# The opening three projections of a hybrid decoder trunk computed pair by pair, and whole-block products pinned in order

## The chip, the cores and the metric

The kernel runs on one core of one Trainium2 chip. The metric is the device time of one execution, in microseconds (us). The engines named here are TensorE (PE for its matmuls, PEld for its weight loads), VectorE (DVE), ScalarE (ACT), GpSimd (POOL) and the engine that issues most DMAs (SP).

## The reference

Four layers, each a token mixer (gated convolution, chunked spatial gating, retention, gated convolution) and a SwiGLU FFN, with RMSNorm ahead of each and at the end. Sequence 512, width 1024, float32. Cut to what matters:

```python
def short_conv_mixer(h, w_in, conv_w, w_out):          # layers 0 and 3
    b_gate, c_gate, z = jnp.split(h @ w_in, 3, axis=-1)
    conv = depthwise_causal_conv3(c_gate * z, conv_w)
    return (b_gate * conv) @ w_out

def swiglu_ffn(h, w_gate, w_up, w_down):
    return (jax.nn.silu(h @ w_gate) * (h @ w_up)) @ w_down

def reference(x, ...):
    for i in range(4):
        x = x + mixer[i % 3](rmsnorm(x, norm_mix_g[i]))
        x = x + swiglu_ffn(rmsnorm(x, norm_ffn_g[i]), ...)
    return rmsnorm(x, final_norm_g)
```

## The kernel before

**Layout.** Activations are held transposed, features on the 128 partitions and the 512 tokens along the free dimension. The residual x is four tiles `x[k]` of 128x1024, each a pair of blocks (two blocks of 128 features, 512 tokens each). So a product over all of x has eight blocks, numbered 0 to 7.

**Split operands.** Every operand is held as a rounded high part and the low remainder. `split` (line 172) makes both: ACT casts the high part, DVE subtracts it from the source for the low part. A product of two operands is three matmuls: high x high, high x low, low x high. `product` (line 182) writes them for a list of blocks into one PSUM bank: for all blocks but the last high x high and high x low, then the weights' low part for all of these, then the three of the last block.

**Two forms of the projections.** A "chunk" of weights covers two blocks of output columns. `columns4` (line 265) computes it by whole blocks: two products of eight blocks, 512 columns, 24 matmuls each. `columns7` (line 220) is a Strassen-like form with seven parts of 256 columns, 12 matmuls each; it needs sums of the blocks of x (`xt`, with parts `th`, `tl`, made in `operand_sums`, line 413) and sums of the weights (`sums`, made in `prepare7`, lines 136 to 139), both made on DVE and split like the rest. The first chunk of each projection in every convolution and FFN is by whole blocks (m = 0; for the FFN the gate `pg` and the up projection `pu`, for the convolution `pc`, `pz` and `pb`), as is one chunk of `pz` at m = 2 of layer 0; the others are seven-part products. The last part of a seven-part product is put off (`self.late`) until `finish` is called.

**Between stages.** `leave` (line 436) computes the eight output blocks of a stage (`out`), adds each to x on DVE (line 457) and at once makes the next stage's operand of it: ACT scales it into `xg` (line 403), `split` makes `xh` and `xl` of it, and for each pair `operand_sums` follows. Squares of x are summed beside it for the norm (lines 318 to 327); the norm's scale itself is applied behind the projections. These temporaries (`xg`, `xt`, the squares) share three buffers (`tmp`).

**Order.** The kernel is written as one stream; a planner of the framework (`schedule_with_timeline_sim=True`) decides at build time, from its own estimate of when each instruction is ready and from priorities, in which order each engine's queue gets its instructions, and which buffer each tile takes. Each engine then works through its queue in that order. `issue_after(ins)` pins what a block of code issues on the engine of `ins` behind `ins`, in issue order alone. `keep_in_program_order` pins the norm's matmuls. Weights are prepared up to four chunks ahead (`weights`, line 147), within four raw buffers, four buffers each for the high and low parts (`wp`), and four more for the parts of the seven-part form that need no sums (`w7`). PSUM has six banks for products (`mm`).

**The opening.** `run` loads x in order and, between its pairs, the weights of the first chunk of `pc` in four pieces (`first_weights`), so that `pc` can begin on the first pair. The chunks of `pz` and `pb` follow by the usual way. The sums of x and the squares follow on ACT behind the last operand (`self.begun`).

Of the kernel before, what the change touches and what calls it, by code (L numbers as in the profile page):

```python
# [11 lines left out]
F32 = mybir.dt.float32  # L12
F32R = mybir.dt.float32r
# [4 lines left out]
P = 128  # L18
# [24 lines left out]
class Kernel:  # L43
    def __init__(self, ctx, tc, a):
        self.tc, self.nc, self.a = tc, tc.nc, a
        pool = lambda name, bufs, **kw: ctx.enter_context(tc.tile_pool(name=name, bufs=bufs, **kw))
        self.const = pool("const", 1)
        self.xp = pool("xp", 1)
        self.opp = pool("opp", 16)
        self.raw = pool("raw", 4)  # L50
        self.wp = pool("wp", 4)
        self.tmp = pool("tmp", 3)
        self.mcp = pool("mcp", 4)
        self.small = pool("small", 1)
        self.mm = pool("mm", 6, space=PSUM)
        self.aux = pool("aux", 1, space=PSUM)
        self.rps = pool("rps", 1, space=PSUM)
        self.chunks, self.ready, self.next = [], {}, 0
        self.late = self.w7 = None
        self.sevens = 2  # L60
        self.held = []

# [53 lines left out]
    def prepare7(self, i):  # L116


        nc = self.nc
        src, _, plain = self.chunks[i]  # L120
        out = [[] for _ in range(8)]
        for half in range(2):
            if plain:
                raw = self.raw.tile([P, 4, NB // 4, P], F32, tag="raw", name=f"raw{i}{half}")
                h, l = (self.wp.tile([P, 4, NB // 4, P], F32R, tag=part, name=f"w{part}{i}{half}") for part in "hl")
                if i:
                    nc.sync.dma_start(raw, src[half])
                    self.split(raw, h, l)
                else:
                    self.first.append((raw, src[half], h, l))  # L130
                for j in range(4):
                    out[j] += [(h[:, j, k], l[:, j, k]) for k in range(NB // 4)]
                continue
            raw = self.raw.tile([P, 4, NB // 4, P], F32, tag="raw", name=f"raw{i}{half}")
            sums = self.sums.tile([P, 4, NB // 4, P], F32, tag="sums", name=f"sums{i}{half}")
            nc.sync.dma_start(raw, src[half])
            nc.vector.tensor_add(sums[:, :2], raw[:, 3:].broadcast_to([P, 2, NB // 4, P]), raw[:, :3:2])  # L137
            nc.vector.tensor_add(sums[:, 2], sums[:, 1], raw[:, 0])
            nc.vector.tensor_add(sums[:, 3], sums[:, 2], raw[:, 1])  # L139
            for x, n, first, pool in ((raw, 3, 0, self.w7), (sums, 4, 3, self.wp)):  # L140
                h, l = (pool.tile([P, n, NB // 4, P], F32R, tag=part, name=f"w{part}{i}{half}{n}") for part in "hl")
                self.split(x[:, :n], h, l)
                for j in range(n):
                    out[first + j] += [(h[:, j, k], l[:, j, k]) for k in range(NB // 4)]
        return out
# [17 lines left out]
        self.next += 1  # L163
        return self.ready.pop(i)

    def first_weights(self, i, j):

        raw, src, h, l = (t[:, j : j + 2] for t in self.first[i])
        self.nc.sync.dma_start(raw, src)
        self.split(raw, h, l)  # L170

    def split(self, src, h, l):

# [8 lines left out]
    def product(self, ps, terms, first=True, last=True, more=False):  # L182


        nc = self.nc
        seq = []
        for lh, ll, rh, rl in terms[:-1]:
            seq += [(lh, rh), (lh, rl)]
        seq += [(ll, rh) for lh, ll, rh, rl in terms[:-1]]
        lh, ll, rh, rl = terms[-1]  # L190
        seq += [(lh, rh), (lh, rl), (ll, rh)]
        for i, (x, y) in enumerate(seq):
            nc.tensor.matmul(  # L193
                ps, x, y, start=first and i == 0, stop=last and i == len(seq) - 1, skip_group_check=more
            )

    def columns(self, name, acts):

# [21 lines left out]
    def columns7(self, name, then, hold=False):  # L220


        nc = self.nc
        w = self.weights()
        c1, c5, c2 = (self.acc(name + n)[:, :H] for n in "152")
        m1, u2, m5 = (self.mcp.tile([P, H], F32, tag="mc", name=name + "m") for i in range(3))
        xs, xt = self.xs, self.xt

        def part(ps, slot, op, at, first):
            at = slice(at * H, (at + 1) * H)  # L230
            self.product(
                ps,
                [(*w[slot][k], o[0][:, at], o[1][:, at]) for k, o in enumerate(op)],
                first,
                more=not first,
            )

        def add(out, ps, m):
            with self.tc.high_priority(SOON):
                nc.vector.tensor_add(out, ps, m)  # L240

        part(c1, 0, xs, 1, True)
        nc.scalar.copy(m1, c1)
        part(c5, 4, xt, 0, True)
        nc.scalar.copy(m5, c5)
        self.finish(hold)
        y = self.temp(name + "y")
        part(c1, 5, xt, 2, False)
        nc.scalar.copy(u2, c1)
        part(c2, 1, xs, 3, True)  # L250
        add(y[:, H : 2 * H], c2, m1)
        part(c5, 6, xs, 2, False)
        add(y[:, :H], c5, u2)
        part(c1, 3, xt, 1, False)
        with self.tc.high_priority(SOON):
            nc.vector.scalar_tensor_tensor(y[:, 2 * H : 3 * H], c1, -1.0, m5, ALU.mult, ALU.subtract)

        def end():
            part(c1, 2, xt, 3, False)
            nc.scalar.mul(y[:, 3 * H :], c1, -1.0)  # L260
            self.held.append(partial(then, y))

        self.late = end

    def columns4(self, name, then, hold=False, kept=True):


        nc = self.nc
        w = self.weights()
        self.finish(hold)  # L270
        out = []
        for even, odd in ((0, 1), (3, 2)):
            ps = self.acc(name)
            terms = []
            for k, (h, l) in enumerate(self.xs):
                terms += [(*w[even][k], h[:, :T], l[:, :T]), (*w[odd][k], h[:, T:], l[:, T:])]
            self.product(ps, terms)
            out.append(ps)
        y = self.hid.tile([P, 2 * T], F32, tag="hid", name=name + "y") if kept else self.temp(name + "y")
        for b in range(2):  # L280
            nc.scalar.copy(y[:, b * T : (b + 1) * T], out[b])
        self.held.append(partial(then, y))

    def finish(self, hold=False):

# [277 lines left out]
        else:  # L563
            self.leave(hid, g, seven)

    def conv(self, j, g, seven, start=False):
        nc = self.nc
        self.r = None
        cw = self.conv_w
# [28 lines left out]
            self.split(y, h, l)  # L598
            acts.extend([(h[:, :T], l[:, :T]), (h[:, T:], l[:, T:])])

        for m in range(NB // 2):
            form = self.columns7 if m else self.columns4
            form("pc", first)
            if m == 3:
# [1 line left out]
            if start and m == 2:  # L606
                form = partial(self.columns4, kept=False)
            form("pz", partial(second, m), m == 0)
            if start and m == 0:
                with self.tc.issue_after(self.begun.ins):  # L610
                    for k in range(NB // 2):
                        self.operand_sums(k, 0)
                    for k in range(NB // 2):
                        self.squares(self.x[k])
            form = self.columns7 if m else self.columns4
            form("pb", third, start and m == 0)
        before = acts[2:]
        begun = [self.begin("out", before) for _ in range(BEGUN)]
        self.finish()
# [217 lines left out]
    def run(self):  # L837
        nc, a = self.nc, self.a
        for i in range(DEPTH):
            j, kind = divmod(i, 3)  # L840
            if kind == 0:
                for m in range(NB // 2):
                    for part in (1, 2, 0):
                        self.plan7(a["conv_w_in"][j, part * NB // 2 + m], m == 0 or (i, m, part) == (0, 2, 2))
                        if m == 3 and part == 1:
# [47 lines left out]
        for _ in range(WARM):  # L893
            nc.tensor.matmul(warm, self.mean_d, self.mean_d, start=True, stop=True)
        nc.scalar.copy(self.const.tile([P, 1], F32, name="first"), self.mean_d[:, :1])
        self.first = []
        self.ready[0] = self.prepare(0)
        for k in range(half):
            if k:
                nc.sync.dma_start(  # L900
                    self.x[k].rearrange("p (b t) -> p b t", b=2),
                    a["x"][2 * k * P : 2 * (k + 1) * P, :].rearrange("(b p) t -> p b t", b=2),
                )
                self.operand(2 * k, 0)
                self.begun = self.operand(2 * k + 1, 0)
                self.first_weights(*((1, 0), (0, 2), (1, 2))[k - 1])
            else:
                for b in range(2):
                    nc.sync.dma_start(self.x[0][:, b * T : (b + 1) * T], a["x"][b * P : (b + 1) * P, :])
                    self.operand(b, 0)  # L910
                    if b == 0:
                        self.first_weights(0, 0)
        nc.sync.dma_start(self.conv_w, a["conv_w"])
        with self.dense():
            self.conv(0, 1, True, True)
            self.ffn(0, 2, False)
        with self.mixed():
            self.sgu(0, 3, True)
# [93 lines left out]
```

## Time and profile before

| what | value |
|---|---|
| median of three runs | 2432.98 us (2431.72 to 2434.72) |
| the profiled execution | 2432.58 us, of which the span is 2430.7 us |
| mean granted TensorE clock | 0.997 of 2.4 GHz |
| PE busy | 2413.3 us, 99% of the span |
| weight loads (PEld) busy | 2166.7 us, 89% |
| DVE busy | 1807.2 us, 74% |
| ACT busy | 1131.8 us, 47% |

The span runs from the first to the last instruction of the one core; all times below are counted from its start. Matmuls overlap, and the busy time of one is longer than its distance to the next, so how fast PE really goes is read from the starts in the timeline and from the counts in a stretch. The granted clock of a stretch is a share of 2.4 GHz; it has two levels, 1.00 and 0.50 (1.2 GHz). An idle time stands in square brackets with what ended it.

### The profile page before, as it was taken

To read this page: it belongs to the slowest core of one execution; us is meant where nothing else is said; L and a number is where in the kernel's file an instruction comes from. 1 tells how busy PE (TensorE), PEld (TensorE's weight loads), DVE (VectorE), ACT (ScalarE), POOL (GpSimd) and SP (SyncE) were. 2 spreads that over 40 slices of the span, in tenths; PEclk is the share of its full clock that TensorE was granted. 3 is DMA by queue.
4 is the path that set the end of the run, shared out by engine and by line. 5 is a ranking of instruction groups with operands and counts; after the bars stand their busy time and mean duration, and the time that the engine had idled before them with its cause. 6 is when DMAs were issued, how large, how long until landed. Compare 5 with 4: busy or idle time off the path is not lost.

```text
span 2430.7 us, 36335 instructions
## 1 busy us (share of the span) xinstructions
PE 2413.3 (99%) x14668; PEld 2166.7 (89%) x14668; DVE 1807.2 (74%) x2617; ACT 1131.8 (47%) x1628; POOL 53.0 (2%) x58
## 2 busy tenths in 40 slices
PE   9999999999999999999999999999999999999998
PEld 8988999988888899999888888899999898899998
DVE  8978978863757888777565464888777897978875
ACT  6545445443324544445433333545445654545444
POOL 0000000000101000000000000000000000000000
PEclk9999999999999999999999999999999999999999
DMA  4232333233333233233222232223233223233231
GB/s 157 93 125 61 118 109 103 88 117 119 96 105 95 74 111 120 87 105 122 91 74 87 74 111 76 95 96 114 91 109 105 87 79 135 73 113 104 91 119 53
DMA packets 79129, 242.02 MB, mean 100 GB/s; under 512 B 8816, under 2 KB 12912, under 8 KB 78960
## 3 DMA queue, kind: packets, MB, share of 16 engines
q1 hardware_dynamic: 77728, 238.61, 30.6%
q8 instruction: 115, 1.88, 0.3%
q10 hardware_dynamic: 1232, 1.09, 0.1%
q14 instruction: 54, 0.44, 0.1%
HBM read 237.56 MB, written 2.10 MB: 99 GB/s over the span
## 4 chain that ended last, share of the span: by engine, by line
PE 96%; DVE 3%; ACT 1%; issue 0%; DMA 0%; SPq 0%; DVEq 0%; ACTq 0%
PE out L193 28%; PE pu L193 22%; PE pg L193 22%; PE pv L193 7%; PE pb L193 3%; PE pc L193 3%; PE pz L193 3%; PE q L193 2%; PE k L193 2%; PE po L193 1%; DVE wl L174 1%; PE ps L697 1%; PE ps L193 1%; DVE x L457 0%; PE rps L384 0%
## 5 line engine op out<-in xcount | busy, mean ns | idle before, releaser
L174 ACT CAST wh<-raw 128x768 fp32r<-128x768 f32 (+3 forms) x502 | 429.2, 861 | 623.8 <-PE out L193 197.3
L174 DVE TENSOR_TENSOR wl<-raw,wh 128x768 fp32r<-128x768 f32 (+3 forms) x502 | 488.5, 985 | 150.4 <-ACT wh L174 147.2
L193 PE MATMUL out<-hidl,wh 128*128 128x512 f32 (+1 forms) x736 | 278.3, 381 | 0.0
L174 ACT CAST wh<-sums 128x1024 fp32r<-128x1024 f32 x194 | 201.1, 1050 | 163.9 <-DVE sums L139 77.9
L193 PE MATMUL out<-hidh,wh 128*128 128x512 f32 (+1 forms) x736 | 274.7, 381 | 0.0
L174 DVE TENSOR_TENSOR wl<-sums,wh 128x1024 fp32r<-128x1024 f32 x194 | 233.7, 1219 | 16.6 <-ACT wh L174 9.2
L193 PE MATMUL out<-hidh,wl 128*128 128x512 f32 (+1 forms) x736 | 204.9, 380 | 0.0
L193 PE MATMUL pg<-xh,wh 128*128 128x256 f32 (+1 forms) x672 | 202.4, 318 | 1.3 <-ACT xh L174 1.3
L193 PE MATMUL pu<-xh,wh 128*128 128x256 f32 (+1 forms) x672 | 200.9, 316 | 0.0
L193 PE MATMUL pg<-xl,wh 128*128 128x256 f32 (+1 forms) x672 | 200.7, 315 | 0.0
L193 PE MATMUL pu<-xl,wh 128*128 128x256 f32 (+1 forms) x672 | 200.1, 314 | 0.0
L457 DVE TENSOR_TENSOR x<-out,x 128x512 f32<-128x512 f32 x192 | 130.5, 685 | 81.2 <-PE out L193 80.9
L193 PE MATMUL pg<-th,wh 128*128 128x256 f32 x640 | 168.6, 284 | 2.5 <-ACT wh L174 2.5
L193 PE MATMUL pg<-tl,wh 128*128 128x256 f32 x640 | 168.7, 284 | 0.0
L193 PE MATMUL pu<-tl,wh 128*128 128x256 f32 x640 | 168.0, 283 | 0.0
L193 PE MATMUL pu<-th,wh 128*128 128x256 f32 x640 | 167.9, 283 | 0.0
L193 PEld LDWEIGHTS out<-hidl,wh 128*128 128x128 f32 x736 | 138.6, 188 | 24.8
L193 PEld LDWEIGHTS out<-hidh,wh 128*128 128x128 f32 x736 | 137.9, 188 | 24.5
L193 PEld LDWEIGHTS out<-hidh,wl 128*128 128x128 f32 x736 | 136.0, 188 | 26.2
L193 PE MATMUL pu<-xh,wl 128*128 128x256 f32 (+1 forms) x672 | 153.2, 313 | 0.0
L193 PE MATMUL pg<-xh,wl 128*128 128x256 f32 (+1 forms) x672 | 149.5, 313 | 0.0
L137 DVE TENSOR_TENSOR sums<-raw 128x512 f32<-128x512 f32 x194 | 130.2, 685 | 15.5 <-DMA raw<-in_ffn_w_up 13.4
(270 smaller groups left out, 5533.6 us busy)
## 6 DMA issues: line engine op xcount, KB each, us to landing
raw<-in_ffn_w_gate SPq DMA_DIRECT2D x88, 512.0 KB, 3.5
raw<-in_ffn_w_up SPq DMA_DIRECT2D x88, 512.0 KB, 3.6
raw<-in_ffn_w_down SPq DMA_DIRECT2D x96, 384.0 KB, 3.3
raw<-in_conv_w_in SPq DMA_DIRECT2D x46, 512.0 KB, 3.9
raw<-in_sgu_w_v SPq DMA_DIRECT2D x16, 512.0 KB, 3.5
raw<-in_sgu_w_u SPq DMA_DIRECT2D x16, 512.0 KB, 3.5
raw<-in_sgu_w_out SPq DMA_DIRECT2D x16, 512.0 KB, 3.5
raw<-in_ret_w_qk SPq DMA_DIRECT2D x16, 512.0 KB, 3.5
```

The lines of the kernel that those rows point to most:

```text
L137: nc.vector.tensor_add(sums[:, :2], raw[:, 3:].broadcast_to([P, 2, NB // 4, P]), raw[:, :3:2])
L174: return self.nc.scalar.copy(h, src), self.nc.vector.tensor_sub(l, src, h.bitcast(F32))
L193: nc.tensor.matmul(ps, x, y, start=first and i == 0, stop=last and i == len(seq) - 1, skip_group_check=more)
L457: nc.vector.tensor_add(x[:, s], ps, x[:, s])
L697: nc.tensor.matmul(ps[:, c * P : (c + 1) * P], v[m // 4][c][:, col], ws[grp // 4][:, at], start=True, stop=True)
```

## The change

The first chunks of the three projections of layer 0 are no longer three `columns4` after one another. A new function, `begin_all`, goes through the four pairs of x; for each it loads the two blocks of x and the three projections' weights of that pair (256 KB each, in runs of 512 bytes), splits them, and adds the pair's contribution to six accumulators, two for each projection: 36 matmuls a pair. For two blocks the matmuls now come as three of the one and three of the other. `blocks_out` copies the accumulators out and holds the follow-up work, as `columns4` did. The sums of x and the squares are issued behind the last operand, as before, from `conv`. The three chunks leave the list of planned weights.

Apart from that, each product of a `columns4` is now pinned on PE behind the product that went before it in the same stage (`self.whole`), across projections, and all parts of the next `columns7` are pinned behind the last of them. This holds wherever `columns4` stands: at the start of the four FFNs and of the convolution of layer 3, and at the one chunk of `pz` in layer 0.

```diff
+    def begin_all(self, srcs):
+        nc = self.nc
+        out = [[self.acc("first") for _ in range(2)] for _ in srcs]
+        parts = []
+        for k in range(NB // 2):
+            half, at = divmod(k, NB // 4)
+            if at == 0:
+                parts = [
+                    [self.wp.tile([P, 4, NB // 4, P], F32R, tag=part, name=f"w{part}f{k}") for part in "hl"]
+                    for _ in srcs
+                ]
...
+            for n, src in enumerate(srcs):
+                raw = self.raw.tile([P, 4, P], F32, tag="raw", name=f"rawf{k}{n}")
+                h, l = (t[:, :, at] for t in parts[n])
+                if n == 0:
+                    for b in range(2):
+                        m = 2 * k + b
+                        nc.sync.dma_start(self.x[k][:, b * T : (b + 1) * T], self.a["x"][m * P : (m + 1) * P, :])
+                        self.begun = self.operand(m, 0)
+                        if b == 0:
+                            nc.sync.dma_start(raw, src[half][:, :, at])
+                            self.split(raw, h, l)
+                else:
+                    nc.sync.dma_start(raw, src[half][:, :, at])
+                    self.split(raw, h, l)
+                xh, xl = self.xs[k]
+                for ps, blocks in zip(out[n], ((0, 1), (3, 2))):
+                    terms = [
+                        (h[:, j], l[:, j], xh[:, b * T : (b + 1) * T], xl[:, b * T : (b + 1) * T])
+                        for b, j in enumerate(blocks)
+                    ]
+                    self.product(ps, terms, k == 0, k == NB // 2 - 1)
+        return out
...
@@ columns7
+        after, self.whole = self.whole, None
+
         def part(ps, slot, op, at, first):
             at = slice(at * H, (at + 1) * H)
-            self.product(
...
+            with self.tc.issue_after(after.ins) if after else nullcontext():
+                self.product(
...
@@ columns4
-            self.product(ps, terms)
+            with self.tc.issue_after(self.whole.ins) if self.whole else nullcontext():
+                self.whole = self.product(ps, terms)
...
@@ conv
-        for m in range(NB // 2):
+        if start:
+            for name, out, then in zip(("pc", "pz", "pb"), start, (first, partial(second, 0), third)):
+                self.blocks_out(name, out, then)
+            with self.tc.issue_after(self.begun.ins):
+                for k in range(NB // 2):
+                    self.operand_sums(k, 0)
+                for k in range(NB // 2):
+                    self.squares(self.x[k])
+        for m in range(1 if start else 0, NB // 2):
...
@@ run
-                for m in range(NB // 2):
+                for m in range(0 if i else 1, NB // 2):
...
-        self.first = []
-        self.ready[0] = self.prepare(0)
-        for k in range(half):
...
-                self.first_weights(*((1, 0), (0, 2), (1, 2))[k - 1])
...
+        first = self.begin_all([a["conv_w_in"][0, part * NB // 2] for part in (1, 2, 0)])
         nc.sync.dma_start(self.conv_w, a["conv_w"])
         with self.dense():
-            self.conv(0, 1, True, True)
+            self.conv(0, 1, True, first)
```

## Rows read from the trace of the kernel before

**Rows 1.** The page's table of busy time, share of the span, instructions.

```profile
PE 2413.3 (99%) x14668; PEld 2166.7 (89%) x14668; DVE 1807.2 (74%) x2617; ACT 1131.8 (47%) x1628; POOL 53.0 (2%) x58
```

**Rows 2.** The page's chain that ended last, by engine.

```profile
PE 96%; DVE 3%; ACT 1%; issue 0%; DMA 0%; SPq 0%; DVEq 0%; ACTq 0%
```

**Rows 3.** PE's timeline, opening: start, duration (us), engine, line, operation, operands, idle before.

```profile
5.61 0.62 PE L193 MATMUL pc<-xh,wh 128*128 128x512 f32 x1
...
10.71 0.50 PE L193 MATMUL pc<-xh,wh 128*128 128x512 f32 x1 [1.00 <-ACT xh L406]
...
42.27 0.28 PE L193 MATMUL pc<-xh,wh 128*128 128x256 f32 x1
42.39 0.28 PE L193 MATMUL pc<-xl,wh 128*128 128x256 f32 x1
```

**Rows 4.** PE's timeline, first FFN's start, up to the norm's matmuls.

```profile
182.35 0.39 PE L193 MATMUL pg<-xh,wh 128*128 128x512 f32 x1
182.58 0.39 PE L193 MATMUL pg<-xl,wh 128*128 128x512 f32 x1
...
211.22 0.95 PE L366 MATMUL scale<-mean_d,sum 128*128 128x1 f32 x8
```

**Rows 5.** Stretches: length, PE, PEld, DVE, ACT, POOL busy (instructions), clock, DMA share, GB/s.

```profile
90.00:100.00 10.00, 10.00 (x75) 9.51 (x74) 7.46 (x11) 4.32 (x7) 0.00 (x0) 1.00 0.05 15
120.00:130.00 10.00, 8.59 (x51) 7.47 (x50) 10.00 (x16) 4.84 (x7) 0.00 (x0) 1.00 0.39 120
182.40:190.30 7.90, 7.89 (x37) 6.25 (x35) 7.17 (x12) 3.97 (x5) 0.00 (x0) 1.00 0.48 139
190.30:193.60 3.30, 1.41 (x7) 1.10 (x8) 2.54 (x5) 3.30 (x6) 0.00 (x0) 1.00 0.52 151
193.60:197.10 3.50, 3.50 (x10) 2.80 (x9) 3.31 (x5) 3.50 (x6) 0.00 (x0) 0.51 0.00 0
2075.00:2081.20 6.20, 4.30 (x13) 3.30 (x13) 5.25 (x8) 6.20 (x9) 0.00 (x0) 0.73 0.27 87
```

**Rows 6.** Timelines of ACT and DVE, first FFN's start: x's scaling, casts, low parts.

```profile
188.27 1.34 ACT L403 ACTIVATE xg<-x,gain 128x512 f32<-128x512 f32 x2 [3.93 <-DVE sum L322]
...
190.45 1.99 ACT L174 CAST wh<-sums 128x1024 fp32r<-128x1024 f32 x2
...
192.99 1.29 DVE L174 TENSOR_TENSOR xl<-xg,xh 128x512 fp32r<-128x512 f32 x2 [0.73 <-ACT xh L174]
...
197.35 0.69 DVE L174 TENSOR_TENSOR xl<-xg,xh 128x512 fp32r<-128x512 f32 x1
...
198.29 0.68 DVE L174 TENSOR_TENSOR xl<-xg,xh 128x512 fp32r<-128x512 f32 x1
```

**Rows 7.** Timelines: a 1024-wide split; other starts: first matmul, last low parts, one cast.

```profile
16.98 1.23 DVE L174 TENSOR_TENSOR wl<-raw,wh 128x1024 fp32r<-128x1024 f32 x1 [0.19 <-ACT wh L174]
...
809.07 0.39 PE L193 MATMUL pg<-xh,wh 128*128 128x512 f32 x1
...
815.55 0.69 DVE L174 TENSOR_TENSOR xl<-xg,xh 128x512 fp32r<-128x512 f32 x1
...
1552.10 0.39 PE L193 MATMUL pg<-xh,wh 128*128 128x512 f32 x1
...
1560.06 1.29 DVE L174 TENSOR_TENSOR xl<-xg,xh 128x512 fp32r<-128x512 f32 x2
...
1897.16 0.39 PE L193 MATMUL pc<-xh,wh 128*128 128x512 f32 x1
...
1900.98 1.06 ACT L174 CAST wh<-raw 128x1024 fp32r<-128x1024 f32 x1 [0.94 <-PE pc L193]
...
1910.68 1.29 DVE L174 TENSOR_TENSOR xl<-xg,xh 128x512 fp32r<-128x512 f32 x2
...
2067.20 0.39 PE L193 MATMUL pg<-xh,wh 128*128 128x512 f32 x1
...
2082.20 0.68 DVE L174 TENSOR_TENSOR xl<-xg,xh 128x512 fp32r<-128x512 f32 x1
```

More of the change, by code (lines that the diff above doesn't have):

```diff
@@ L59, in __init__ @@
         self.late = self.w7 = None
+        self.whole = None
         self.sevens = 2
@@ L125, in prepare7 @@
                 h, l = (self.wp.tile([P, 4, NB // 4, P], F32R, tag=part, name=f"w{part}{i}{half}") for part in "hl")
[L126 to L130, printed above, removed]
+                nc.sync.dma_start(raw, src[half])
+                self.split(raw, h, l)
                 for j in range(4):
@@ L164, in weights, with blocks_out @@
         return self.ready.pop(i)
[L166 to L170, printed above, removed]
+    def begin_all(self, srcs):
[9 more added lines that the diff above has]
+                ]
+            xs = []
+            for n, src in enumerate(srcs):
[11 more added lines that the diff above has]
+                    nc.sync.dma_start(raw, src[half][:, :, at])
+                    self.split(raw, h, l)
+                xh, xl = self.xs[k]
[6 more added lines that the diff above has]
+        return out
+    def blocks_out(self, name, out, then, kept=True):
+        y = self.hid.tile([P, 2 * T], F32, tag="hid", name=name + "y") if kept else self.temp(name + "y")
+        for b in range(2):
+            self.nc.scalar.copy(y[:, b * T : (b + 1) * T], out[b])
+        self.held.append(partial(then, y))
     def split(self, src, h, l):
@@ L192, in product @@
         for i, (x, y) in enumerate(seq):
-            nc.tensor.matmul(
+            mm = nc.tensor.matmul(
                 ps, x, y, start=first and i == 0, stop=last and i == len(seq) - 1, skip_group_check=more
             )
+        return mm
     def columns(self, name, acts):
@@ L227, in columns7 @@
         xs, xt = self.xs, self.xt
+        after, self.whole = self.whole, None
         def part(ps, slot, op, at, first):
             at = slice(at * H, (at + 1) * H)
-            self.product(
[L232 to L236, printed above, removed]
+            with self.tc.issue_after(after.ins) if after else nullcontext():
+                self.product(
+                    ps,
+                    [(*w[slot][k], o[0][:, at], o[1][:, at]) for k, o in enumerate(op)],
+                    first,
+                    more=not first,
+                )
         def add(out, ps, m):
@@ L276, in columns4 @@
                 terms += [(*w[even][k], h[:, :T], l[:, :T]), (*w[odd][k], h[:, T:], l[:, T:])]
-            self.product(ps, terms)
+            with self.tc.issue_after(self.whole.ins) if self.whole else nullcontext():
+                self.whole = self.product(ps, terms)
             out.append(ps)
[L279 to L282, printed above, removed]
+        self.blocks_out(name, out, then, kept)
     def finish(self, hold=False):
@@ L564, in ffn, with conv @@
             self.leave(hid, g, seven)
-    def conv(self, j, g, seven, start=False):
+    def conv(self, j, g, seven, start=()):
         nc = self.nc
@@ L608, in conv @@
             form("pz", partial(second, m), m == 0)
[L609 to L614, printed above, removed]
             form = self.columns7 if m else self.columns4
-            form("pb", third, start and m == 0)
+            form("pb", third)
         before = acts[2:]
@@ L895, in run @@
         nc.scalar.copy(self.const.tile([P, 1], F32, name="first"), self.mean_d[:, :1])
-        self.first = []
-        self.ready[0] = self.prepare(0)
-        for k in range(half):
[L899 to L905, printed above, removed]
-                self.first_weights(*((1, 0), (0, 2), (1, 2))[k - 1])
[L907 to L912, printed above, removed]
+        first = self.begin_all([a["conv_w_in"][0, part * NB // 2] for part in (1, 2, 0)])
         nc.sync.dma_start(self.conv_w, a["conv_w"])
         with self.dense():
-            self.conv(0, 1, True, True)
+            self.conv(0, 1, True, first)
             self.ffn(0, 2, False)
```

## The prediction

> **What bounds the kernel now.** I read the page's busy table first: TensorE (PE) is busy 99% of the span [rows 1]; the chain that ended last is 96% PE [rows 2]. So the kernel's time is PE's work plus the places where PE stands. A busy PE can hide lost time, so I then read PE's own timeline for the distance between starts: 512-column matmuls follow each other every 0.227 us (182.35 to 182.58), 256-column ones every 0.120 us (42.27 to 42.39) [rows 3, 4]. Against that pace the lost time lies in few places. (1) The opening: 144 whole-block matmuls (three projections of 48) run from 5.61 to 42.27 us, 36.66 us, where 144 x 0.2267 = 32.64 would do, so 4.0 us are lost; the largest hole is 1.00 us at 10.71, waiting for x [rows 3]. (2) From 120 to 130 us PE is busy 8.59 of 10 [rows 5]. (3) The start of the first FFN (stage "F0"): from 182.35 to the norm's matmuls at 211.22 are 28.87 us for 96 whole-block and 24 part matmuls, 96 x 0.2267 + 24 x 0.120 = 24.64, so 4.2 us are lost [rows 4]. In 190.30 to 193.60 PE is busy only 1.41 us, and behind it, 193.60 to 197.10, the granted clock is 0.51, that is 1.2 instead of 2.4 GHz [rows 5]. (4) The last FFN ("F3") repeats this near 2075 to 2081 (4.30 us busy of 6.20, mean clock 0.73) [rows 5], and I price it alike. The starts of the FFNs of layers 1 and 2 ("F1", "F2") and of layer 3's convolution ("C3") lose nothing now.
>
> **Why those starts go well now.** Each whole-block product needs the eight blocks of x in turn: 14 matmuls (high x high, high x low) for blocks 0 to 6, then 7 of the weights' low part, then three for block 7. The blocks of the new x leave DVE and ACT late. In F0 PE begins at 182.35 [rows 4], but the low parts of blocks 4 and 5 start on DVE at 192.99, of block 6 at 197.35 and of block 7 at 198.29 [rows 6]. PE bridges these 16 us because the planner lets it take from all four products (two gate, two up) whatever block is there, then parts of the next seven-part product; 37 matmuls run in 182.40 to 190.30 [rows 5]. The lateness is DVE's and ACT's: DVE is busy 7.17 of those 7.90 us [rows 5], and ACT's scaling of blocks 4 and 5 at 188.27 had waited 3.93 us for a temporary that a DVE sum holds [rows 6].
>
> **The change, part by part.**
>
> *Opening.* The loads go pair by pair, and each pair of x feeds 36 matmuls (8.2 us) instead of 12, so after the first pair PE no longer waits for x. The first matmul needs the same two 256 KB loads and stays at 5.61. I leave 0.5 us of waits in the first pair and take 3.5 of the 4.0 us at the end of this block. Added: weights split in twelve 512-wide pieces instead of four such and four 1024-wide ones; with 0.68 us per 512-wide subtraction [rows 6] and 1.23 per 1024-wide one [rows 7] DVE does 12 x 0.68 - 4 x 0.68 - 4 x 1.23 = 0.5 us more, beside PE. The sums of x for the seven-part form start only when x's last pair is in, and wait on ACT behind its scaling; queued behind them on ACT and DVE are the next chunk's weights. SP's later weight loads stand behind x and the twelve small loads; PE has 8 us of work per pair to cover these. Further on DVE decides: it is busy all 10 us of 120 to 130, where PE stands 1.4 us, and idle 2.5 us in 90 to 100 [rows 5]. So the gain lies between 0 and 4.0 us; I take 2.8, since DVE's idle time ahead of its dense stretch can move forward with PE.
>
> *Products in order.* No instruction is added; the pins fix PE's issue order. Behind a matmul that waits for block 4 now stand all later whole products and the seven-part product, and PE has nothing else. The first product covers 14 + 7 = 21 matmuls, 4.8 us, before it needs block 7, and 13 matmuls, 2.9 us, before block 6's low part. If the blocks come when they come now, the first product ends 0.23 us (its low part) + 7 x 0.227 + 3 x 0.227 = 2.5 us after block 6's low part, and the others follow without stop, since their blocks are all there.
> - F0: block 6 is written at 197.35 + 0.69 = 198.04 [rows 6], the first product ends at 200.6 instead of 182.35 + 24 x 0.2267 = 187.8: 12.8 us late. The 4.2 us lost now go, so +8.6.
> - F1: begins 809.07; block 7's low part is written at 815.55 + 0.69 = 816.24, needed at 809.07 + 22 x 0.2267 = 814.06: +2.2 [rows 7].
> - F2: begins 1552.10; blocks 6 and 7 start on DVE at 1560.06 as a pair of 1.29, so block 6 is done by 1560.7, product at 1563.2 instead of 1557.5: +5.7 [rows 7].
> - C3: begins 1897.16; the pair starts at 1910.68, block 6 done by 1911.4, product at 1913.9 instead of 1902.6: +11.3 [rows 7].
> - F3: begins 2067.20; block 6 done at 2082.88 [rows 7]: 12.8 late, less 4.2: +8.6.
>
> These sum to 36.4 us. Less what the new order moves out of the operands' way: in F0 ACT casts two weight sums, 1.99 us, at 190.45 just ahead of blocks 4 and 5 [rows 6]; they can start because the spread-out order frees weight buffers early, and will now come later, -2.0 each in F0 and F3. In C3 ACT's cast at 1900.98 (1.06 us) has waited for PE's pc [rows 7] and its subtraction of 1.23 follows; -2.3. Together 30.1 us. From below these waits cost nothing (blocks within 2.9 and 4.8 us; then F0's and F3's 4.2 us each are gained), from above 36.4; I stay near the top, since the rows of DVE and ACT that make the blocks late don't depend on PE's order, but for the casts named.
>
> *Clock.* The drop in F0 came right behind 3.30 us in which PE was busy 1.41 [rows 5]. Four starts (F0, F2, C3, F3) would now stand 5 to 12 us with still less work. One such stretch of 3.5 us at half clock costs 1.7 us of matmul time; I take one for each start, 4 x 1.7 = 6.8 (the drops of today are inside the 4.2 us already subtracted). Bounds: 0, if the slow stretch falls where PE waits anyway, and two stretches each, 13.6. The Trainium skill (TensorE: Matmul & The Clock Gate, section "What's actually happening") says that the slow clock is the default and that only sustained activity releases it, so an order that makes PE stand pays again when it resumes. By that rule the four drops are certain, as in F0's row; without it the sum would be 6.8 us lower.
>
> **Sum.** -2.8 + 30.1 + 6.8 = +34.1 us on the profiled execution's 2432.6, which is 0.4 below the median of the three runs: 2466.7 us.
>
> **Rivals.**
> - *The blocks arrive in time* (faster). All engines are planned anew; if with PE's demand in order the planner puts x's blocks ahead of the weights' preparation, the holes of F0 and F3 go and none comes: -2.8 - 8.4 = -11.2, 2421.4 us. It decides at 2.9 us for block 6 and 4.8 us for block 7 after the first matmul of the stage. For it: F1 misses it by only 2.2 us. Against it: F0 misses by 12.8 us, with DVE nearly full and ACT held by a buffer, which no pin on PE frees.
> - *Half as late.* The moved casts let the blocks come with half the delay: (12.8 + 2.2 + 5.7 + 11.3 + 12.8) / 2 = 22.4, less 8.4 lost today, less 2.8, and 1.7 of clock in F0 and F3: +14.6, 2447 us. For it: both engines have other work between the blocks that could slip. Against it: that work was ready and will be again.
> - *Nothing measurable.* Late blocks cost F1 and F2 together some 8 us, F0 and F3 gain 4.2 each, and C3's blocks come in time; with the opening lost to DVE the total stays within 5 us of 2433. Against it: C3 is 11.3 us short.
>
> **How the numbers follow.** Chances: forecast 0.70, blocks in time 0.13, half as late 0.12, nothing 0.05. A measurement of this kernel can tell about 0.2% (5 us) from no change. Faster by more: 0.13; within: 0.05; slower: 0.82. The range reaches from below the half-late case (2440) to the top of the bounds (36.4 + 6.8 + some of the second clock stretch: 2480).
>
> **What would show it.** In the new trace: pb's last whole matmul near 38.8 us at the earliest; at each stage start one tile alone (pg or pc) in a run of 24, with holes up to several us that end on xh or xl; a half-clock stretch behind the holes of F0, F2, C3 and F3; the norm's matmuls of F0 and F3 later after the last out matmul than today's 28.9 us. I am wrong if x's low parts of blocks 6 and 7 are written within 5 us of the stage's first matmul, if PE fills the holes with other tiles, or if the opening loses more than 4 us.

## The result and the profile after

| | before | after |
|---|---|---|
| median of four runs each | 2433.24 us | 2474.78 us (2472.46 to 2476.07) |
| the profiled execution / its span | 2432.58 / 2430.7 us | 2472.46 / 2470.7 us |
| mean granted clock | 0.997 | 0.989 |

The changed kernel takes 1.017 times as long, 95% interval 1.0152 to 1.0187: 41.5 us more on the medians, 40.0 us on the two spans. In the numbers below a stage's "loss" is the time from its first whole-block matmul to the norm's `scale` matmul, less the counted matmuls in between at 0.2267 us for each of 512 columns and 0.120 us for each of 256. In the changed kernel `product`'s matmuls stand at line 229, `split` at 210, x's scaling at 441, the squares at 359 and 360.

The page's busy line, then its chain that ended last, by engine; they answer to [rows 1, 2]:

```profile
PE 2422.6 (98%) x14668; PEld 2169.6 (88%) x14668; DVE 1814.1 (73%) x2621; ACT 1135.4 (46%) x1632; POOL 54.1 (2%) x58
...
PE 92%; DVE 5%; issue 1%; ACT 1%; DMA 1%; DVEq 0%; SPq 0%; ACTq 0%
```

The same matmuls, but DVE's share of the chain has gone from 3 to 5% and PE's from 96 to 92%: PE waits. Where, PE's timeline shows (start, duration, operation, idle time before with what ended it): the opening, the first FFN's start and its end at the norm's matmuls, answering to [rows 3, 4].

```profile
6.26 0.73 PE L229 MATMUL first<-xh,whf 128*128 128x512 f32 x2 [1.15 <-ACT whf L210]
...
38.92 0.39 PE L229 MATMUL first<-xh,wlf 128*128 128x512 f32 x1
39.15 0.28 PE L229 MATMUL pc<-xh,wh 128*128 128x256 f32 x1
...
178.91 0.39 PE L229 MATMUL pg<-xh,wh 128*128 128x512 f32 x1
...
181.37 0.50 PE L229 MATMUL pg<-xl,wh 128*128 128x512 f32 x1 [1.16 <-DVE xl L210]
...
187.20 0.80 PE L229 MATMUL pg<-xh,wh 128*128 128x512 f32 x1 [4.72 <-ACT xh L210]
189.00 0.80 PE L229 MATMUL pg<-xl,wh 128*128 128x512 f32 x1 [1.01 <-DVE xl L210]
...
191.84 0.80 PE L229 MATMUL pg<-xh,wh 128*128 128x512 f32 x1 [1.19 <-ACT xh L210]
193.08 0.79 PE L229 MATMUL pg<-xl,wh 128*128 128x512 f32 x1 [0.45 <-DVE xl L210]
193.67 2.62 PE L229 MATMUL pg<-xh,wl 128*128 128x512 f32 x7
...
216.04 0.62 PE L404 MATMUL scale<-mean_d,sum 128*128 128x1 f32 x5
```

The opening is denser: 144 whole-block matmuls lie between 6.26 and 39.15, 32.89 us, where 36.66 were needed. In the first FFN ("F0") one product, `pg`, goes from block to block and stands five times, 8.5 us in all, each time until ACT or DVE writes the next block. The stage takes 216.04 - 178.91 = 37.13 us instead of 28.87, a loss of 12.5 instead of 4.2. The last FFN ("F3") has the same holes at the same distances from its start (4.72 us at 2106.28).

Next, stretches: length, busy time (instructions) of PE, PEld, DVE, ACT and POOL, granted clock, DMA share and GB/s. First DVE's two stretches of the opening as in [rows 5], then F0's holes and what follows, the fourth stage named "C3", and F3:

```profile
90.00:100.00 10.00, 10.00 (x82) 9.85 (x81) 10.00 (x13) 6.99 (x11) 0.00 (x0) 1.00 0.05 15
120.00:130.00 10.00, 10.00 (x73) 9.40 (x72) 10.00 (x16) 5.29 (x8) 0.00 (x0) 1.00 0.40 132
...
181.70:195.40 13.70, 6.33 (x14) 3.43 (x13) 12.60 (x21) 8.64 (x13) 0.00 (x0) 0.63 0.17 57
186.50:192.00 5.50, 2.61 (x5) 1.28 (x5) 5.50 (x8) 5.12 (x9) 0.00 (x0) 0.50 0.00 0
195.40:198.90 3.50, 3.50 (x17) 2.86 (x16) 2.98 (x5) 3.05 (x5) 0.00 (x0) 0.99 0.00 0
...
1914.00:1931.00 17.00, 7.79 (x15) 4.03 (x16) 16.24 (x26) 10.94 (x16) 0.00 (x0) 0.55 0.29 93
...
2098.00:2115.00 17.00, 8.47 (x21) 4.92 (x20) 15.90 (x25) 10.04 (x14) 0.00 (x0) 0.66 0.26 83
```

From 181.70 to 195.40 PE issues 14 matmuls while DVE is busy 12.60 of 13.70 us, and the clock is 0.63 in the mean. Of its two levels 0.50 must then have held for (1 - 0.63) / 0.5 x 13.7 = 10.1 us; from 186.50 to 192.00 it is 0.50 throughout, and a matmul behind a wait there lasts 0.80 us, where the one at 181.37, ahead of the slow stretch, lasts 0.50. Once PE has work again (195.40 on), it is back at 0.99.

What the holes wait for, on ACT and DVE, in F0 (answering to [rows 6]), F1, F2 and C3 (answering to [rows 7]); each "x2" is blocks 6 and 7, or 4 and 5, together:

```profile
184.36 1.33 ACT L441 ACTIVATE xg<-x,gain 128x512 f32<-128x512 f32 x2 [2.55 <-DVE sum L360]
185.60 1.03 ACT L210 CAST th<-xt 128x1024 fp32r<-128x1024 f32 x1
186.53 1.13 ACT L210 CAST xh<-xg 128x512 fp32r<-128x512 f32 x2
...
188.26 1.29 DVE L210 TENSOR_TENSOR xl<-xg,xh 128x512 fp32r<-128x512 f32 x2
...
192.34 1.29 DVE L210 TENSOR_TENSOR xl<-xg,xh 128x512 fp32r<-128x512 f32 x2
...
820.30 0.69 DVE L210 TENSOR_TENSOR xl<-xg,xh 128x512 fp32r<-128x512 f32 x1
...
1567.13 1.29 DVE L210 TENSOR_TENSOR xl<-xg,xh 128x512 fp32r<-128x512 f32 x2
...
1911.56 0.39 PE L229 MATMUL pc<-xh,wh 128*128 128x512 f32 x1
...
1923.60 1.33 ACT L441 ACTIVATE xg<-x,gain 128x512 f32<-128x512 f32 x2 [3.47 <-DVE sum L360]
...
1927.50 1.28 DVE L210 TENSOR_TENSOR xl<-xg,xh 128x512 fp32r<-128x512 f32 x2
```

In F0 no cast of weight sums stands ahead of x's blocks any more (ACT goes from `th` at 185.60 straight to `xh` at 186.53), and the wait for the buffer that a sum of squares holds is 2.55 instead of 3.93 us. Block 6's low part is written 192.34 + 0.69 - 178.91 = 14.1 us after the stage's first matmul (before 15.7). In C3 it comes 1927.50 + 0.69 - 1911.56 = 16.6 us after it (before 14.2), behind a wait of 3.47 us for a squares' buffer that the kernel before does not have there.

The losses by stage, in us:

| stage | before | after | difference | forecast |
|---|---|---|---|---|
| up to F0 (opening) | - | - | -3.4 | -2.8 |
| F0 | 4.2 | 12.5 | +8.3 | +8.3 |
| F1 | 0 | 2.4 | +2.4 | +2.2 |
| F2 | 0 | 7.4 | +7.4 | +7.4 |
| C3 | 0 | 16.0 | +16.0 | +10.7 |
| F3 | 4.2 | 13.7 | +9.5 | +8.3 |
| sum | | | +40.2 | +34.1 |

The opening's entry is the start of F0, 178.91 for 182.35. The forecast of F2 is 5.7 and 1.7 for the clock, of C3 11.3 - 2.3 + 1.7, of F0 and F3 8.6 - 2.0 + 1.7 each.

### The profile page after: what moved, and what is told of

The parts are those of the page before. It is cut to its first block, busy times and chain, and to the rows that moved or that the text cites. A ratio compares the mean times of both kernels' runs of the same rounds, so it can differ in the third digit from the quotient of the medians.

```text
span 2470.7 us, 36371 instructions
## 1 busy us (share of the span) xinstructions
PE 2422.6 (98%) x14668; PEld 2169.6 (88%) x14668; DVE 1814.1 (73%) x2621; ACT 1135.4 (46%) x1632; POOL 54.1 (2%) x58
## 4 chain that ended last, share of the span: by engine, by line
PE 92%; DVE 5%; issue 1%; ACT 1%; DMA 1%; DVEq 0%; SPq 0%; ACTq 0%
PE out L229 27%; PE pu L229 22%; PE pg L229 21%; PE pv L229 7%; PE pz L229 3%; PE pb L229 2%; PE pc L229 2%; PE q L229 2%; PE k L229 2%; DVE wl L210 2%; PE first L229 1%; PE po L229 1%; PE ps L737 1%; DVE x L495 1%; PE ps L229 1%
## 5 line engine op out<-in xcount | busy, mean ns | idle before, releaser
L210 ACT CAST wh<-raw 128x768 fp32r<-128x768 f32 (+3 forms) x494 | 422.8, 862 | 633.0 <-PE out L229 205.3
L210 DVE TENSOR_TENSOR wl<-raw,wh 128x768 fp32r<-128x768 f32 (+3 forms) x494 | 481.8, 987 | 142.8 <-ACT wh L210 138.0
L229 PE MATMUL pg<-xl,wh 128*128 128x256 f32 (+1 forms) x672 | 204.0, 318 | 10.9 <-DVE xl L210 10.9
L229 PEld LDWEIGHTS pg<-xh,wh 128*128 128x128 f32 x672 | 129.2, 192 | 23.5 <-ACT xh L210 16.1
```

The costliest lines, as they stand in the source:

```text
L210: return self.nc.scalar.copy(h, src), self.nc.vector.tensor_sub(l, src, h.bitcast(F32))
L229: mm = nc.tensor.matmul(ps, x, y, start=first and i == 0, stop=last and i == len(seq) - 1, skip_group_check=more)
```

## The experiments

The theory: the opening gains some 3 us; the pins cost some 37, because x's blocks come when ACT and DVE make them and PE has nothing beside. The rivals: that the new opening itself brings the loss into the later stages, that the pin on the seven-part product costs as much as the chain of whole products, and that the slow clock makes up more of it than forecast.

### The opening alone

```diff
-            with self.tc.issue_after(self.whole.ins) if self.whole else nullcontext():
-                self.whole = self.product(ps, terms)
+            self.product(ps, terms)
```

> The new opening with no pins on whole products or on seven-part products. Theory (late blocks): the pins alone cost, at the five later stage starts; the opening alone brings what PE gained up to the first FFN in the changed kernel, 182.1 - 178.7 = 3.4 us, and F0 and F3 lose their 4.2 us as before: about 2430 us, 0.14% faster. Rival (the opening): the smaller loads and the later sums of x make DVE and ACT late in the whole first layer and the planner orders all later stages anew, so that a good part of the loss stays: 2440 us or more.

Measured: 2427.73 us, ratio 0.9982 (0.9973 to 0.9991), 3.7 us below the kernel before on this chip. Losses: F0 2.2, F1 and F2 0, C3 0.5, F3 3.7. The opening is a gain, and the whole of the loss is the pins'. In F0 block 6 is written 15.2 us after the first matmul, 1.1 us later than with the pins (14.1), and yet PE works through it. F0 and F3 were expected to lose 4.2 each as before: F3's start has a half-clock stretch as in the kernel before, F0's has none.

### The pins alone

The kernel before with `self.whole` in `columns4` and `columns7`, its own opening kept. The three first chunks of that opening are `columns4`, so here they are pinned too.

```diff
-            self.product(ps, terms)
+            with self.tc.issue_after(self.whole.ins) if self.whole else nullcontext():
+                self.whole = self.product(ps, terms)
```

> The kernel before with the pins alone: whole products in order, the next seven-part product behind them, the opening as it was. Theory (late blocks): all of the loss and none of the opening's gain: 2474.8 + 3.4 = 2478 us, with holes at the starts of F0, F1, F2, C3, F3. Rival (the opening): within some 10 us of 2433.

Measured: 2474.85 us, ratio 1.0177 (1.0163 to 1.0191), +43.4 us. Losses: F0 13.1, F1 2.4, F2 7.4, C3 12.7, F3 13.8. The 144 matmuls of the opening end at 44.87 instead of 42.27, and F0 begins 1.2 us later than in the kernel before (182.35), which is the pins' price in the old opening; the changed kernel has no `columns4` there and does not pay it:

```profile
183.51 0.39 PE L194 MATMUL pg<-xh,wh 128*128 128x512 f32 x1
```

Without it the two parts make 43.4 - 1.2 - 3.7 = 38.5, against 41.5 for both. What does not add is C3, 12.7 here and 16.0 with the opening.

### The seven-part product behind the whole ones, these free

```diff
-            with self.tc.issue_after(after.ins) if after else nullcontext():
+            with ExitStack() as order:
+                for mm in after or []:
+                    order.enter_context(self.tc.issue_after(mm.ins))
...
-                self.whole = self.product(ps, terms)
+            self.whole = [*(self.whole or []), self.product(ps, terms)]
```

> The new opening; whole products free among themselves, the next seven-part product still pinned behind the last matmul of each of them. Theory (the order among whole products costs): PE can draw on four products for each block that is there (six at C3), so F1, F2 and C3 lose nothing, and F0 and F3 lose 4.2 us as before and about 1 us each for the seven matmuls of the seven-part product that filled the hole before: about 2432 us. Rival (what stands behind them costs, the seven-part product being the filler): near 2470 us.

Measured: 2430.31 us, ratio 0.9993 (0.9984 to 1.0003). Against the opening alone, on the same chip, it costs 2.6 us: F0 loses 4.6 instead of 2.2, F3 4.5 instead of 3.7, the others nothing. Part of that is the clock: in F0 this kernel has a half-clock stretch of 3.4 us that the opening alone does not have (first line this kernel, second line the opening alone):

```profile
190.40:193.80 3.40, 3.40 (x10) 2.63 (x9) 3.21 (x5) 3.40 (x5) 0.00 (x0) 0.50 0.00 0
...
190.40:193.80 3.40, 3.40 (x19) 2.89 (x18) 3.21 (x5) 3.40 (x6) 0.00 (x0) 1.00 0.00 0
```

As long as four products can take any block that is there, the seven-part product as filling is worth only these 2.6 us.

### The chain of whole products alone, the seven-part product free

```diff
-        after, self.whole = self.whole, None
+        after = self.whole = None
```

> The new opening; whole products pinned one behind the other, the seven-part product free. Theory (the order among whole products costs): the first seven-part product can give at most two parts of 12 matmuls, 2.9 us a stage, and needs the same late blocks, so most of the loss stays: 2462 to 2475 us. Rival (the pin of the seven-part product costs): near 2432 us.

Measured: 2475.61 us, ratio 1.0177 (1.0163 to 1.0191). Losses: F0 13.3, F1 3.9, F2 8.6, C3 16.7, F3 12.5. The stretch of F0 with the holes (columns as above):

```profile
179.00:196.00 17.00, 8.48 (x20) 4.91 (x19) 15.76 (x24) 10.30 (x14) 0.00 (x0) 0.63 0.25 79
```

20 matmuls in 17 us: though it was free to, no seven-part product went into F0's holes; its first 24 matmuls come only behind the last whole product, and the two parts that were expected to fit did not come. So the chain alone is enough for the whole loss, and the second pin adds nothing to it. Why the planner left the free product behind was not tried.

### With the pins, the squares behind the last operand

For a stage with whole products ahead, ACT's squares of x are issued behind the scaling of block 7, so that they hold no temporary while the blocks are made.

```diff
-                    self.operand(m, g, seven)
+                    mul = self.operand(m, g, seven)
...
-            if final and m % 2:
+            if final and m % 2 and not seven:
                 self.squares(x)
+        if final and seven:
+            with self.tc.issue_after(mul.ins):
+                for x in self.x:
+                    self.squares(x)
```

> The changed kernel, pins and all; where the next stage is a dense one, the squares of x are issued on ACT behind the last block's scaling instead of between the pairs. Theory (blocks late because of DVE and ACT, the shared temporaries among it): a square no longer takes the temporary that the scaling of blocks 4 and 6 waits for, and its sums of 1.22 us leave DVE ahead of the blocks; block 6's low part comes 3 to 6 us earlier and the loss at F0 and F3 falls from 12.5 and 13.7 us to 7 to 10, with something at F2 and C3: 2455 to 2468 us. Rival (DVE's other work steps in): block 6 within 1 us of where it was, 2472 us or more.

Measured: 2462.17 us, ratio 1.0124 (1.011 to 1.0138). Against the changed kernel the ratio falls by 0.0046, 11 us. The losses: F0 11.3, F1 3.9, F2 2.0, C3 13.2, F3 11.4. Block 6 comes 12.2 us after the first matmul in F0 (14.1), 0.1 in F2 (8.6), 13.2 in C3 (16.6). So the squares do hold the blocks back, most in F2. The time is in the expected range by F2 and C3; in F0 and F3, where block 6 was to come 3 to 6 us earlier and the loss to fall to 7 to 10, this step of the theory missed: block 6 comes 1.9 us earlier. In F0 another temporary takes the squares' place: the scaling of blocks 4 and 5 waits no longer 2.55 us for a sum of squares, but 2.06 us for the sums of x (`tl`), as ACT's timeline shows:

```profile
180.56 1.33 ACT L441 ACTIVATE xg<-x,gain 128x512 f32<-128x512 f32 x2 [2.06 <-DVE tl L210]
```

### The opening, no pins, the squares behind the last operand

The edits of the first and the fifth experiment together.

> The new opening with no pins, and the squares behind the last block's scaling. Theory: the blocks come earlier, so the 2.2 us of F0 and the 3.7 us of F3 that the opening alone still loses go, with F3's half-clock stretch: 2422 to 2424 us. Rival (DVE's other work steps in): 2427 to 2428 us, like the opening alone.

Measured: 2424.39 us, ratio 0.9966 (0.9954 to 0.9979): faster than the kernel before by 7.5 us and than the changed one by 50. Losses: F0 and F3 1.0 each, the others 0. The page's chain by engine, and the stretch of F0:

```profile
PE 98%; DVE 1%; ACT 1%; issue 0%; DVEq 0%; POOL 0%; ACTq 0%; POOLq 0%
...
180.00:209.00 29.00, 28.87 (x153) 24.33 (x151) 25.52 (x38) 19.67 (x27) 0.00 (x0) 1.00 0.20 68
```

PE is busy 28.87 of 29.00 us at full clock, although DVE is busy 25.52 of them and block 6 comes 14.5 us after the first matmul, no earlier than with the pins (14.1). So what counts most is whether PE may go round the late blocks. Against the opening alone the blocks do come earlier, blocks 4 and 5 by 2.8 us and block 6 by 0.7 (10.9 and 15.2 there), as the theory had it; the loss falls to 1.0 and not to nothing, and the time is 0.4 us above the expected range.

### With the pins, the waits filled with matmuls whose results are not read

42 extra matmuls into a spare bank in F0 and in F3, 24 in F2, 54 in C3, put between those of the first product where it waits; in these products every matmul is also pinned behind the one before it.

```diff
+            for _ in range(fill.get(i, 0)):
+                with self.tc.issue_after(mm.ins):
+                    mm = nc.tensor.matmul(spare, seq[0][0], seq[0][1], start=True, stop=True)
```

> The changed kernel; into the waits of the first whole product of F0, F2, C3 and F3 go 42, 24, 54 and 42 matmuls whose results nothing reads, slightly fewer than fit, so that PE stays busy while the blocks are as late as before. Theory: the waits stay, the half-clock stretches go, and what they cost goes with them: lost time beyond the waits for block 6 is 1.3 us at F0, 1.7 at F2, 2.3 at C3 and 2.5 at F3, so 7.8 us less: about 2467 us, clock 1.00 throughout these starts. Rival (the slow clock falls where PE waits anyway): 2474 us or more.

Measured: 2466.00 us, ratio 1.014 (1.0125 to 1.0156), 0.0030 or 7.3 us below the changed kernel. The two 95% intervals overlap slightly (up to 1.0156 here, from 1.0152 there), so the price is read from the stages too. The filled stretches of F0, F2, C3 and F3:

```profile
181.80:195.10 13.30, 13.01 (x53) 9.30 (x52) 12.20 (x19) 8.65 (x13) 0.00 (x0) 1.00 0.15 49
1563.00:1570.00 7.00, 7.00 (x31) 5.51 (x31) 6.77 (x11) 2.08 (x3) 0.00 (x0) 1.00 0.63 217
1911.00:1929.00 18.00, 17.75 (x75) 13.20 (x75) 17.23 (x27) 11.73 (x17) 0.00 (x0) 1.00 0.28 87
2095.80:2109.00 13.20, 12.94 (x53) 9.15 (x52) 12.10 (x19) 8.68 (x13) 0.00 (x0) 1.00 0.17 54
```

The clock is 1.00 in all four, and the blocks come when they came (block 6 in F0 14.1 us after the first matmul, in C3 16.4 for 16.6). From the first matmul to the norm's the stages are shorter by 1.1 (F0), 0 (F1), 1.5 (F2), 2.4 (C3) and 2.3 us (F3), together 7.3. This is the price of the slow clock, but for some 0.3 us in C3 by which the block is earlier. The five starts lose 43.6 us more than before (8.3 + 2.4 + 7.4 + 16.0 + 9.5); the other 36 are waiting alone. The Trainium skill (TensorE: Matmul & The Clock Gate, section "What's actually happening") has it that the clock is throttled by default and that activity releases the throttle; that the filled stretches stay at 1.00 agrees.

### The opening, no pins, the other choice of buffer pool

Weights of output columns are put into one of two pools by the parity of their place in the list of planned weights. The new opening takes three chunks off that list, so every later place changes its parity. This kernel turns it back.

```diff
-        pool = self.w7 if self.w7 and n <= 6 * P and i % 2 == 0 else self.wp
+        pool = self.w7 if self.w7 and n <= 6 * P and i % 2 == 1 else self.wp
```

> The new opening with no pins; the rule that gives every other chunk of output weights the second buffer pool is shifted by one, since the three chunks that left the list turned it over for all later stages. Theory on C3 (its blocks came 2.4 us later after the stage's start than in the kernel before because the output weights there swapped pools, not because of the pins): block 6's low part is written about 14.2 us after C3's start instead of 16.4, C3 loses nothing, and the time stays within 2 us of the opening alone. Rival (something else of the opening): still near 16.4 us.

Measured: 2427.75 us, ratio 0.9982 (0.9973 to 0.9991), as the opening alone. But C3's blocks move. Each fence: the stage's first matmul and the low parts of blocks 6 and 7, here, in the opening alone, and in the pins alone (which have the old list):

```profile
1892.06 0.39 PE L229 MATMUL pc<-xh,wh 128*128 128x512 f32 x1
...
1905.53 1.29 DVE L210 TENSOR_TENSOR xl<-xg,xh 128x512 fp32r<-128x512 f32 x2
```

```profile
1892.42 0.39 PE L229 MATMUL pc<-xh,wh 128*128 128x512 f32 x1
...
1908.16 1.28 DVE L210 TENSOR_TENSOR xl<-xg,xh 128x512 fp32r<-128x512 f32 x2
```

```profile
1916.96 0.39 PE L194 MATMUL pc<-xh,wh 128*128 128x512 f32 x1
...
1929.64 1.28 DVE L175 TENSOR_TENSOR xl<-xg,xh 128x512 fp32r<-128x512 f32 x2
```

With 0.69 us for one block: 14.2, 16.4 and 13.4 us after the first matmul. So the pools that the shorter list turned over make C3's blocks late, and the changed kernel, which has that list, has them at 16.6. With PE free this costs nearly nothing (C3 loses 0.5 without the edit, 0 with it). With the pins it is some 3 us, 16.0 against 12.7 in the second experiment, which has the old list but also the old opening; the pins with the new opening and the pools turned back were not tried. In F0 too the edit takes block 6 back from 15.2 to 15.7 us, where the kernel before has it. How the other pool leads to the 3.47 us that ACT waits for a squares' buffer there was not tried; the squares moved back take the delay away too (13.2, fifth experiment).

## Why the prediction held

Slower was right, the range held the time, and the forecast of 2466.7 was 8 us short of 2474.78. By its steps:

- **Opening, -2.8; it gave -3.4.** The end of the 144 matmuls was forecast for 38.8 at the earliest and is 39.15. The first matmul did not stay at 5.61 but came at 6.26; hardly 0.25 us are lost behind it (32.89 for 32.64), where I had left 0.5, so the block ends 0.4 us later than I took. DVE, which I feared further on, had its dense stretch earlier, as I had thought it could: in 90 to 100 it is now busy 10.00 us instead of 7.46, and in 120 to 130 PE no longer stands [rows 5]. That hole, though, had ended on ACT's cast of weights, and not on DVE (PE's timeline, kernel before):

```profile
129.62 0.38 PE L193 MATMUL pz<-th,wh 128*128 128x256 f32 x1 [1.41 <-ACT wh L174]
```

- **Products in order, 36.4 less 6.3.** The way the blocks decide the end of the first product is right: F1 2.4 (2.2), F2 7.4 (5.7 and the clock), F0 8.3 (8.3). That F0 agrees to the tenth is luck in part: the blocks gained 1.6 us and not 2.0, and the clock cost 1.1 and not 1.7. F3, priced like F0, came out 1.2 higher; its clock cost 2.3. The fourth experiment shows that the chain of the whole products is enough, and that the pin on the seven-part product is not needed for the loss. I had named both as one.
- **Casts out of the way, -2.0 in F0 and F3.** They did go, and the blocks came 1.6 us earlier. Not all of it is the casts': with the pins and the old list of weights block 6 is at 14.6 for 15.7, so 1.1; the other 0.5 comes with the shorter list (15.2 in the opening alone, 15.7 with the pools turned back).
- **C3, forecast +10.7, measured +16.0: this step failed.** I took 2.3 us off for a cast. With the old list of weights the pins bring the block only 0.8 us earlier (13.4 for 14.2, second experiment): the cast is gone, but ACT then stands longer for a load of weights ahead of x's scaling, 4.86 us there for 3.17 in the kernel before (ACT's timelines, in this order):

```profile
1925.08 0.83 ACT L175 CAST wh<-raw 128x768 fp32r<-128x768 f32 x1 [4.86 <-DMA raw<-in_conv_w_in]
...
1905.21 0.84 ACT L174 CAST wh<-raw 128x768 fp32r<-128x768 f32 x1 [3.17 <-DMA raw<-in_conv_w_in]
```

  And with the list of the changed kernel it comes 2.4 us later, at 16.6 where I took 14.2 - 2.3 = 11.9. The three chunks that leave the list stand in the diff; I read what the opening gained by that, but overlooked that the choice of pools depends on the place in the list. That is 4.7 of the 5.3 us missing, the clock the rest.
- **Clock, 6.8; measured 7.3.** The sum holds, the picture does not, so its closeness is luck. The slow stretches are two to five times as long as the 3.5 us I took (6.8 us in F2, 10.2 in F0, 13.7 in F3, 17.1 in C3), and the greater part of each lies ahead of the end of the last hole, where it costs little, instead of behind the holes. And the price is not one for each stage: 1.1 in F0, 2.4 in C3.
- **Rivals.** The blocks in time and half as late: neither came; F0's block 6 is written 14.1 us after the first matmul, where the first rival needed 2.9 and the second some 9. Nor did the third: C3's blocks, which it needed in time, came later than before. Without the chain F0's loss does go down, to 2.2 us and with the squares moved to 1.0; this is the gain that the first rival priced, by another way than it said.

## What to carry to other kernels

Where the operands of several independent accumulations come late and one by one, do not fix their order on the engine: the free order lost 0 to 4 us at each start and the fixed one 2 to 16, with the operands made at nearly the same times. Before a list loses entries, look for rules that go by a place in it (a parity, a modulus); here a choice of buffers turned over and moved operands by 2 us some 1700 us later in the kernel. And a temporary that is needed only at the end (the squares) should not hold the buffers of those needed first: moved back, it was worth 3 us without the pins and 11 with them.

## What was not expected of the hardware

The same hole can cost the clock or not. In F1 the last low part is late by nearly the same time in the changed kernel and in the fifth experiment (PE's timeline):

```profile
821.05 0.50 PE L229 MATMUL pg<-xl,wh 128*128 128x512 f32 x1 [2.08 <-DVE xl L210]
```

```profile
819.71 0.80 PE L229 MATMUL pg<-xl,wh 128*128 128x512 f32 x1 [2.07 <-DVE xl L210]
```

Behind it the first runs on at full speed and loses 2.4 us, the second at half and loses 3.9, and so does the fourth experiment behind the same hole. It happens within one kernel as well: in the opening alone F0 and F3 have their blocks at the same times (block 6 at 15.2 us), and F0 runs through at 1.00 and loses 2.2 us, F3 has a half-clock stretch of 3.4 us and loses 3.7:

```profile
2073.50:2076.90 3.40, 3.40 (x11) 2.65 (x10) 3.22 (x5) 3.40 (x5) 0.00 (x0) 0.50 0.00 0
```

What decides between them no run here tells.

In its first 8 us the new opening, whose weights come in runs of 512 bytes, moves less. The traffic before and after:

```profile
DMA packets 1161, 1.95 MB, mean 244 GB/s; under 512 B 226, under 2 KB 226, under 8 KB 1161
```

```profile
DMA packets 2234, 1.61 MB, mean 201 GB/s; under 512 B 232, under 2 KB 1878, under 8 KB 2234
```

All eight traces with this opening lie between 1.55 and 1.69 MB, the two with the old one at 1.80 and 1.95. SP's queue shows longer issues as well, for x too, whose transfers are the same (0.60 for 0.43 us), here after:

```profile
1.23 0.65 SPq L187 DMA_DIRECT2D rawf<-in_conv_w_in  x1
1.93 0.60 SPq L184 DMA_DIRECT2D x<-in_x  x1
```

Whether the issues or the short runs make this was not tried apart. It is not what makes the first matmul late. In the changed kernel ACT's first cast of weights waits 1.08 us for its transfer and starts at 5.59 instead of 4.96, and the first matmul comes 0.65 us later; but in the other seven traces with the same loads the first matmul starts between 5.33 and 5.99, in the opening alone before that of the old kernel (5.61):

```profile
5.44 0.50 PE L229 MATMUL first<-xh,whf 128*128 128x512 f32 x1
```

And in all eight the 144 matmuls end between 38.9 and 39.3 us, whenever the first one starts. So the time of the first matmul does not set the opening's gain.
